# Turning the attention probabilities with VectorE and a trip through memory, in place of TensorE

## The chip, the core and the metric

The kernel runs on one core of a Trainium2 chip. The core has TensorE (PE, matmuls, with the loading of weights shown apart as PEld), VectorE (DVE), ScalarE (ACT), GpSimd (POOL) and SyncE (SP), which here only issues DMAs. Each engine works through its own list of instructions in the order in which they stand; semaphores hold an instruction until what it reads is there. The metric is the device time of one execution in microseconds. Comparisons are made between runs on one chip.

## The reference, cut to what matters

One encoder layer on 512 tokens of width 2048: a modulated RMS norm, one input projection, two token mixers side by side (attention with 16 heads of 64, and a gated linear attention), gates, an output projection, and a last RMS norm. The change touches the attention alone. For each head the reference forms logits, a softmax, and a product with the values:

```
s = jnp.einsum('bnqrhe,bnkrhe->bhrnqk', qb, kw).astype(jnp.float32) * (E ** -0.5)
...
m = jnp.max(s, axis=-1, keepdims=True)
p = jnp.exp(s - m)
den = jnp.sum(p, axis=-1, keepdims=True)
o = jnp.einsum('bhrnqk,bnkrhe->bhrnqe', (p / den).astype(v.dtype), vw)
```

The three dilated patterns are merged with weights from their denominators. The kernel does this with one dense 512 by 512 table per head: the bias table `g` holds, for each distance, the shared bias and the log of how many patterns reach it, so one softmax over all 512 keys gives the merged result.

## The kernel before, in words

All matrices are float32, kept as a high part and a low part (float32r), and each product is three matmuls (L169 to L171). The projection runs in units of 512 output columns. A unit reads eight weight groups of 512 KB (`raw`, four slots, L286); ACT makes the high part of each (L313), DVE the low part (L297), and PE runs 192 matmuls of 128x128 on 128x512 per unit, 24 per group.

Four units, `qk2`, `qk4`, `qk6` and `gk`, carry the attention beside their own matmuls: `unit` takes a list of side items with a place between 0 and 1, and emits each between the unit's matmuls when that share of them is out; items at 1 or more go to the next unit. So PE's list is written out by hand (PE is scheduled manually). The lists of DVE, ACT, POOL and SP are ordered by the framework's scheduler from the order of emission and its own view of when things are ready, side items first.

Each of these units does four heads, each head four tiles of 128 queries against 512 keys, so 16 tiles per unit and 64 in all. Names in the program carry head and tile: `p62` is head 6, tile 2; two tiles make a half, `pt50` and `o50` are head 5, half 0. A tile goes through these steps:

- score: two matmuls `s` on PE (L576, L577); DVE adds the bias row `g` and takes the row minimum (L580, CUSTOM_DVE_ANT in the profile, ISA in the program's list, with a second short row that reads the minimum out); ACT takes the exponential and its sum (L583); DVE the reciprocal (L584); POOL scales the row (L585).
- turn, two tiles later: four PE transposes into PSUM (`t`, L597); ACT makes the high part (L601) and DVE the low part (L602) of the turned tile in `pt`.
- values, per half: eight matmuls `o` on PE (L611); ACT copies one part out (L614); DVE adds the two into `cat` (L618).

At the end of such a unit `qk_evict` (L531) takes the new heads' queries and keys out of PSUM: eight ACT copies and eight DVE operations of 64x512 (L540, L550), and eight small DMAs. `g_load` fetches a head's bias table through SP (L564). `some_sums` puts conditioning sums of 128x1024 (L244, L680) and their loads beside the matmuls; 8 of the 48 lie in `qk6` and `gk`. Pools: `t2` has 16 tiles of 128x512 (queries, keys and score tiles), `b8` eight of 8 KB a row, `pa` three PSUM banks shared by `s`, `t` and `o`.

## Time and profile before

| | |
|---|---|
| median of 3 runs | 957.51 us (955.98 to 957.8) |
| profiled execution | 959.9 us, of which the span from first to last instruction is 957.9 us |
| granted clock | 0.997 |
| PE busy | 939.7 us, 98% of the span |
| DVE, ACT, POOL busy | 605.3, 431.5, 81.1 us |
| the units qk2, qk4, qk6, gk | 191.9 to 257.3, to 323.0, to 390.3, to 457.5 us |

In the profile's timeline a row gives start, duration, engine, line, operation, output and inputs, shape, and in brackets the idle time before it with what ended it. Groups of instructions give the count, the busy time in all, the mean in ns of one, and the idle time before them. The view by windows gives each engine's busy time in a stretch. Durations of operations that follow each other on one engine overlap a little, so the distance of two starts is what one costs its engine.

### The profile page before, as it was taken

To read this page: it belongs to the slowest core of one execution; us is meant where nothing else is said; L and a number is where in the kernel's file an instruction comes from. 1 tells how busy PE (TensorE), PEld (TensorE's weight loads), DVE (VectorE), ACT (ScalarE), POOL (GpSimd) and SP (SyncE) were. 2 spreads that over 40 slices of the span, in tenths; PEclk is the share of its full clock that TensorE was granted. 3 is DMA by queue.
4 is the path that set the end of the run, shared out by engine and by line. 5 is a ranking of instruction groups with operands and counts; after the bars stand their busy time and mean duration, and the time that the engine had idled before them with its cause. 6 is when DMAs were issued, how large, how long until landed. Compare 5 with 4: busy or idle time off the path is not lost.

```text
span 957.9 us, 11999 instructions
## 1 busy us (share of the span) xinstructions
PE 939.7 (98%) x4464; PEld 777.1 (81%) x4464; DVE 605.3 (63%) x900; ACT 431.5 (45%) x719; POOL 81.1 (8%) x100
## 2 busy tenths in 40 slices
PE   8999999999999999999999999999999999999996
PEld 5888788888888888888778888888887888888884
DVE  7988899675756676766435656675964352546421
ACT  5443533565655655655215544543834152233222
POOL 0000000012122022122000000000010000202120
PEclk9999999999999999999999999999999999999998
DMA  9999687443333463533454244354555464244013
GB/s 330 413 411 365 229 296 275 150 131 105 112 103 105 144 200 108 173 127 103 150 176 146 86 132 154 132 176 154 173 195 183 132 221 154 92 151 152 23 55 121
DMA packets 45180, 163.76 MB, mean 171 GB/s; under 512 B 5730, under 2 KB 6018, under 8 KB 40386
## 3 DMA queue, kind: packets, MB, share of 16 engines
q1 hardware_dynamic: 44946, 162.68, 49.9%
q8 instruction: 35, 0.57, 0.2%
q10 hardware_dynamic: 176, 0.33, 0.1%
q14 instruction: 23, 0.18, 0.1%
HBM read 154.51 MB, written 4.28 MB: 166 GB/s over the span
## 4 chain that ended last, share of the span: by engine, by line
PE 84%; DMA 6%; DVE 5%; issue 3%; ACT 1%; SPq 0%; POOL 0%; ACTq 0%; DVEq 0%; POOLq 0%
PE ps_o L170 6%; PE ps_o L169 6%; PE ps_o L171 6%; DMA rawg<-in_wg 6%; PE ps_qk L170 5%; PE ps_qk L169 5%; PE ps_qk L171 5%; PE o L611 3%; PE sta L169 3%; PE sta L170 3%; PE sta L171 3%; PE stb L171 3%; PE stb L169 3%; PE stb L170 3%; PE ps_gv L171 3%; PE ps_gv L170 3%
## 5 line engine op out<-in xcount | busy, mean ns | idle before, releaser
L585 POOL TENSOR_SCALAR p<-p,st 128x512 f32<-128x512 f32 x64 | 45.5, 711 | 406.6 <-DVE st L584 357.9
L244 DVE CUSTOM_DVE_ANT_0 cb<-cb,sb,c_bcond 128x2048 f32<-128x2048 f32 (+1 forms) x32 | 73.4, 2294 | 0.0
L583 ACT ACTIVATE p<-p,st 128x512 f32<-128x512 f32 x64 | 46.1, 721 | 56.8 <-DVE st L580 56.3
L602 DVE TENSOR_TENSOR pt<-t,pt 128x512 fp32r<-128x512 f32 x64 | 44.0, 689 | 16.2 <-ACT pt L601 15.8
L580 DVE CUSTOM_DVE_ANT_0 p<-s,g 128x512 f32<-128x512 f32 x64 | 43.6, 687 | 14.8 <-PE s L577 14.5
L601 ACT ACTIVATE pt<-t 128x512 fp32r<-128x512 f32 x64 | 37.8, 592 | 10.2 <-PE t L597 9.2
L244 DVE CUSTOM_DVE_ANT_0 rawg<-rawg,sb,gate 128x1024 f32<-128x1024 f32 x16 | 20.5, 1283 | 29.6 <-DMA rawg<-in_wg 29.6
L611 PEld LDWEIGHTS o<-pt,vv 128*128 128x128 f32 x256 | 34.7, 188 | 5.0 <-DVE pt L602 2.2
L597 PEld LDWEIGHTS t<-c_ident,p 128*128 128x128 f32 x256 | 31.8, 140 | 8.5
L597 PE MATMUL t<-c_ident,p 128*128 128x128 f32 x256 | 38.3, 272 | 0.0
L611 PE MATMUL o<-pt,vv 128*128 128x256 f32 x256 | 36.6, 283 | 0.9 <-DVE pt L602 0.8
L244 DVE CUSTOM_DVE_ANT_0 rawg<-rawg,sb,c_bcond 128x1024 f32<-128x1024 f32 x16 | 20.5, 1283 | 26.3 <-DMA rawg<-in_wg 26.3
L1014 POOL TENSOR_TENSOR x<-x,fgain 128x512 f32<-128x512 f32 x12 | 20.3, 1696 | 185.3 <-ACT ysq L1012 185.3
L1012 ACT ACTIVATE ysq<-x 128x512 f32<-128x512 f32 x16 | 10.1, 632 | 47.2 <-DVE x L1010 47.2
L767 POOL TENSOR_SCALAR dc<-st,sc 128x256 f32<-128x256 f32 x16 | 10.4, 652 | 245.5 <-DVE st L764 240.6
L1009 DVE TENSOR_TENSOR y<-ps_o,sb 128x512 f32<-128x512 f32 x16 | 10.9, 684 | 25.9 <-PE ps_o L171 25.9
L584 DVE RECIPROCAL st<-st 128x1 f32<-128x1 f32 x64 | 10.3, 162 | 24.9 <-ACT p L583 24.9
L576 PE MATMUL s<-ks,qs 128*128 128x512 f32 x64 | 25.1, 391 | 0.0
L577 PE MATMUL s<-kl,qs 128*128 128x512 f32 x64 | 25.0, 391 | 0.0
L774 ACT ACTIVATE sq<-st,sc 128x256 f32<-128x256 f32 x24 | 12.2, 509 | 26.8 <-DVE st L769 14.3
L1010 DVE TENSOR_TENSOR x<-y,x 128x512 f32<-128x512 f32 x16 | 18.0, 1125 | 0.3
L614 ACT ACTIVATE oh<-o 64x256 f32<-64x256 f32 x32 | 12.2, 382 | 13.0 <-PE o L611 12.2
(1275 smaller groups left out, 2916.7 us busy)
## 6 DMA issues: line engine op xcount, KB each, us to landing
cb<-in_wm SPq DMA_DIRECT2D x31, 1024.0 KB, 7.9
rawg<-in_wg SPq DMA_DIRECT2D x32, 512.0 KB, 3.4
raw_o<-in_w_o SPq DMA_DIRECT2D x32, 512.0 KB, 3.4
raw_qk<-in_w_qk SPq DMA_DIRECT2D x24, 512.0 KB, 3.4
rawb<-in_w_sb SPq DMA_DIRECT2D x16, 512.0 KB, 4.8
rawv<-in_wv SPq DMA_DIRECT2D x16, 512.0 KB, 3.8
raw_gv<-in_w_gv SPq DMA_DIRECT2D x16, 512.0 KB, 3.5
raw_ag<-in_w_ag SPq DMA_DIRECT2D x16, 512.0 KB, 3.3
```

The lines of the kernel that those rows point to most:

```text
L169: mm(ps, lh, rh, start=first, stop=False)
L170: mm(ps, ll, rh, start=False, stop=False)
L171: mm(ps, lh, rl, start=False, stop=last)
L244: nc.vector.tensor_tensor_reduce(out=w, in0=w, in1=with_, op0=ALU.mult, op1=ALU.add, scale=1.0, scalar=init, accum_out=dst)
L576: mm(ps, qs[:, q], ks, start=True, stop=False)
L580: nc.vector.tensor_tensor_reduce(out=t, in0=ps, in1=gt[h][:, P * i:P * i + 512], op0=ALU.add, op1=ALU.min, scale=1.0, scalar=3e38, accum_o ...
L583: act(t, t, AF.Exp, bias=st[:, 0:1], scale=-1.0, accum_out=st[:, 1:2])
L585: nc.gpsimd.tensor_scalar(t, t, st[:, 2:3], 1.0, op0=ALU.mult, op1=ALU.mult)
L597: nc.tensor.transpose(pk[:, kt * P:kt * P + P], t[:, kt * P:kt * P + P], ident)
L601: act(hi, src, AF.Copy)
L602: tt(lo, src, hi.bitcast(F32), op=ALU.subtract)
L611: mm(po[:, :256], vv[h // 4][:, kt, h % 4, :], t[:, w, kt, :], start=kt == 0 and w == 0, stop=kt == 3 and w == 1)
```

## The change

The turn on PE is taken out. `score` ends after the exponential; `scale` does the reciprocal and POOL's scaling. `turn` is now one VectorE transpose per tile (L602 of the changed kernel, STREAM_TRANSPOSE in the program's list), which turns each 32x32 block in its place and sorts the blocks by key range. `leave` writes the tile to a scratch buffer in memory (`away`, 256 KB); `back` reads a half back with four DMAs that put each block row on its partitions (`pf`, 512 KB, in a `raw` slot, in runs of 512 bytes). `parts` makes high and low parts of a whole half (128x1024) from `pf`, and `values` follows as before.

Each step has its own place: with x the number of the tile in the unit, score at x, scale x + 0.45, turn x + 0.9, leave x + 1.5, and for the half that ends with x, back x + 2.9, parts x + 4.6, values x + 7.0; one step of x is 0.0555 of a unit, from 0.13 on. So the last values of a unit fall into the next one. Beside it, the 8 sums leave `qk6` and `gk` (3 more in `gv0`, 3 in `gv1`, 1 in `ag0`, 1 in `gg1`), the weights are fetched one group less ahead in these four units, `cat` is allotted later, the row of shifts moves from 0.05 to 0.6 of `qk6`, and a small tensor `lrs` is split into two tiles of `t2`.

```diff
--- before.py
+++ after.py
@@ -70,12 +70,12 @@
 
 
 
-ATT_AT = (0.17, 0.8, 0.04, 0.05, 0.05)
+ATT_AT = (0.13, 0.0555)
 
 GLA_AT = (0.01, 0.02, 0.33, 0.46, 0.46, 0.56, 0.64, 0.76, 0.76, 0.88)
 GLA_FIRST = 0.2
 
-SUMS_IN = {"qk6": 4, "gk": 4, "gv0": 9, "gv1": 2, "ag0": 7, "ag1": 9, "gg0": 9}
+SUMS_IN = {"gv0": 12, "gv1": 5, "ag0": 8, "ag1": 9, "gg0": 9}
 
 
 def _plan(tasks, free, ready):
@@ -556,7 +556,7 @@
     def attention(pairs):
 
         tiles = [(2 * p + j, i) for p in pairs for j in range(2) for i in range(4)]
-        gt, pt, pr_ = {}, {}, {}
+        gt, pt, pr_, away, pf = {}, {}, {}, {}, {}
         heads = [2 * p + j for p in pairs for j in range(2)]
 
         def g_load(h):
@@ -566,8 +566,6 @@
 
         def score(h, i):
             def go():
-                if h % 8 == 0 and i == 0:
-                    cat[h // 8] = B8(f"cat{h // 8}", [4, 512])
                 if i == 1 and h != heads[-1]:
                     g_load(h + 1)
                 qs, ks, kl, _ = stacks[h]
@@ -581,29 +579,59 @@
                     out=t, in0=ps, in1=gt[h][:, P * i:P * i + 512], op0=ALU.add, op1=ALU.min,
                     scale=1.0, scalar=3e38, accum_out=st[:, 0:1])
                 act(t, t, AF.Exp, bias=st[:, 0:1], scale=-1.0, accum_out=st[:, 1:2])
+                pr_[h, i] = t, st
+            return go
+
+        def scale(h, i):
+
+            def go():
+                t, st = pr_.pop((h, i))
                 nc.vector.reciprocal(st[:, 2:3], st[:, 1:2])
                 nc.gpsimd.tensor_scalar(t, t, st[:, 2:3], 1.0, op0=ALU.mult, op1=ALU.mult)
+                half, ii = divmod(i, 2)
+                if ii == 0:
+                    away[h, half] = dp.tile([2, P, 512], F32, tag=f"away{h}{half}", name=f"away{h}{half}")
                 pr_[h, i] = t
             return go
 
         def turn(h, i):
+
+
             def go():
-                half, ii = divmod(i, 2)
-                if ii == 0:
-                    pt[h, half] = B8(f"pt{h}{half}", [2, 4, 256], F32R)
-                t = pr_.pop((h, i))
-                pk = PA(f"t{h}{i}")
-                for kt in range(4):
-                    nc.tensor.transpose(pk[:, kt * P:kt * P + P], t[:, kt * P:kt * P + P], ident)
-                hi = pt[h, half][:, 0, :, P * ii:P * ii + P]
-                lo = pt[h, half][:, 1, :, P * ii:P * ii + P]
-                src = pk.rearrange("p (k q) -> p k q", k=4)
+                t = T2(f"pt{h}{i}")
+                nc.vector.transpose(t.rearrange("p (b k r) -> p k b r", b=4, k=4), pr_.pop((h, i)))
+                pr_[h, i] = t
+            return go
+
+        def leave(h, i):
+            def go():
+                nc.sync.dma_start(away[h, i // 2][i % 2], pr_.pop((h, i)))
+            return go
+
+        def back(h, half):
+
+            def go():
+                t = away.pop((h, half))
+                f = RAW(f"pf{h}{half}", [8, 128])
+                for b in range(4):
+                    nc.sync.dma_start(f[32 * b:32 * b + 32], bass.AP(
+                        t.tensor, t.offset + P * b, [[512, 32], [32 * 512, 8], [1, P]]))
+                pf[h, half] = f
+            return go
+
+        def parts(h, half):
+            def go():
+                t = pt[h, half] = B8(f"pt{h}{half}", [2, 4, 256], F32R)
+                src = pf.pop((h, half)).rearrange("p b (k r) -> p k b r", k=4)
+                hi, lo = [t[:, e].rearrange("p k (b r) -> p k b r", b=8) for e in range(2)]
                 act(hi, src, AF.Copy)
                 tt(lo, src, hi.bitcast(F32), op=ALU.subtract)
             return go
 
         def values(h, half):
             def go():
+                if h % 8 == 0 and half == 0:
+                    cat[h // 8] = B8(f"cat{h // 8}", [4, 512])
                 t = pt.pop((h, half))
                 po = PA(f"o{h}{half}")
                 for kt in range(4):
@@ -620,20 +648,21 @@
 
         items = []
         n = len(tiles)
-        for x in range(n + 4):
-            if x < n:
-                items.append(score(*tiles[x]))
-            if 2 <= x <= n + 1:
-                items.append(turn(*tiles[x - 2]))
-            if 3 <= x <= n + 2 and tiles[x - 3][1] % 2 == 1:
-                items.append(values(tiles[x - 3][0], tiles[x - 3][1] // 2))
+        for x in range(n):
+            if True:
+                items.append((x, score(*tiles[x])))
+                items.append((x + 0.45, scale(*tiles[x])))
+                items.append((x + 0.9, turn(*tiles[x])))
+                items.append((x + 1.5, leave(*tiles[x])))
+                if tiles[x][1] % 2 == 1:
+                    h, half = tiles[x][0], tiles[x][1] // 2
+                    items.append((x + 2.9, back(h, half)))
+                    items.append((x + 4.6, parts(h, half)))
+                    items.append((x + 7.0, values(h, half)))
+        items.sort(key=lambda v: v[0])
         g_load(heads[0])
-        start, span, move0, move1, move_last = ATT_AT
-        at = [start + (q + 0.5) / len(items) * span for q in range(len(items))]
...
-        return list(zip(at, items))
+        start, step = ATT_AT
+        return [(start + step * x, go) for x, go in items]
 
     def gate_half(m, z):
 
@@ -854,7 +883,7 @@
                 todo = list(range(gi[name, gorder[0] if name == "o3" else 0], upto[name, g] + 1))
                 for i in todo:
                     split_hi(i)
-                for ahead in (1, 2):
+                for ahead in (1, 2)[:1 if name[:2] in ("qk", "gk") else 2]:
                     fetch(upto[name, g] + ahead)
             if i0 not in low:
                 split_lo(i0)
@@ -900,27 +929,29 @@
     for p in range(2):
         qk_evict(p, psb["b", 4 + 2 * p], psb["b", 5 + 2 * p])
     for n, p in (("qk2", 0), ("qk4", 2), ("qk6", 4)):
-        ps = unit(n, False, attention((p, p + 1)) + ([(0.05, shift_row)] + some_sums(n) if p == 4 else []))
+        ps = unit(n, False, attention((p, p + 1)) + ([(0.6, shift_row)] if p == 4 else []))
         for q in range(2):
             qk_evict(p + 2 + q, ps[2 * q], ps[2 * q + 1])
 
-    ps = unit("gk", False, attention((6, 7)) + some_sums("gk"))
+    ps = unit("gk", False, attention((6, 7)))
     gla["k"] = B8("gkt", [4, 512])
     for i in range(4):
         act(gla["k"][:, i, :], ps[i], AF.Copy)
 
 
-    lrb = B8("lrb", [KT, 32])
+    lrb = T2("lrb").rearrange("p (k c) -> p k c", k=KT)
     nc.sync.dma_start(lrb, a["w_lr"][0])
-    lrs = B8("lrs", [KT, 2, 32], F32R)
-    act(lrs[:, :, 0, :], lrb, AF.Copy)
-    tt(lrs[:, :, 1, :], lrb, lrs[:, :, 0, :].bitcast(F32), op=ALU.subtract)
+    lrs = [T2(f"lrs{e}", F32R).rearrange("p (k e c) -> p k e c", k=8, e=2) for e in range(2)]
+    for e in range(2):
+        src = lrb[:, 8 * e:8 * e + 8, :]
+        act(lrs[e][:, :, 0, :], src, AF.Copy)
+        tt(lrs[e][:, :, 1, :], src, lrs[e][:, :, 0, :].bitcast(F32), op=ALU.subtract)
     plr = PA("plr")
 
     def lr_tick(n):
         if n % 2 == 1:
             k = n // 2
-            w = lrs[:, k, :, :].rearrange("p a b -> p (a b)")
+            w = lrs[k // 8][:, k % 8, :, :].rearrange("p a b -> p (a b)")
             mm(plr[:64], w, h_hi[:, k, :], start=k == 0, stop=False)
             mm(plr[:64], w, h_lo[:, k, :], start=False, stop=k == KT - 1)
 
```

Three places of the lists show what moved. First DVE in the middle of `qk4`, around head 6 (the numbers behind the names only tell buffers apart). Before:

```order
L580 ISA p62_2502,st62_2503<-s62_2499,g6_2332 128x512
L580 ISA st62_2503 128x1
L297 TENSOR_TENSOR qk47l_2607<-raw_qk47_2437,qk47h_2606 128x1024
L584 RECIPROCAL st62_2503<-st62_2503 128x1
L602 TENSOR_TENSOR pt60_2511<-t60_2512,pt60_2511 128x4x128
L618 TENSOR_TENSOR cat0_1549<-o51_2527,oh51_2536 64x256
L580 ISA p63_2549,st63_2550<-s63_2546,g6_2332 128x512
L580 ISA st63_2550 128x1
L584 RECIPROCAL st63_2550<-st63_2550 128x1
L602 TENSOR_TENSOR pt60_2511<-t61_2558,pt60_2511 128x4x128
L580 ISA p70_2571,st70_2572<-s70_2568,g7_2472 128x512
```

and with the change:

```order
L628 TENSOR_TENSOR pt41_2410<-pf41_2356,pt41_2410 128x1024
L578 ISA p62_2512,st62_2513<-s62_2509,g6_2332 128x512
L578 ISA st62_2513 128x1
L646 TENSOR_TENSOR cat0_1774<-o41_2497,oh41_2506 64x256
L297 TENSOR_TENSOR qk46l_2458<-raw_qk46_2383,qk46h_2457 128x1024
L589 RECIPROCAL st62_2513<-st62_2513 128x1
L602 STREAM_TRANSPOSE pt62_2532<-p62_2512 128x4x4x32
```

which is followed at once by

```order
L578 ISA p63_2537,st63_2538<-s63_2534,g6_2332 128x512
L578 ISA st63_2538 128x1
L589 RECIPROCAL st63_2538<-st63_2538 128x1
L602 STREAM_TRANSPOSE pt63_2567<-p63_2537 128x4x4x32
L628 TENSOR_TENSOR pt50_2484<-pf50_2416,pt50_2484 128x1024
L646 TENSOR_TENSOR cat0_1774<-o50_2569,oh50_2578 64x256
L578 ISA p70_2584,st70_2585<-s70_2581,g7_2465 128x512
```

Before, between the minimum of a tile and the next tile's stands the reciprocal and the low part of a tile that is two tiles older. With the change the tile's own transpose stands there, which reads what POOL has scaled after this reciprocal; `pt41` and `pt50` (L628) are the low parts of whole halves, and `cat` of `o50` stands right behind `pt50`.

Second PE at the same place. Before:

```order
L170 MATMUL ps_qk4_3_2147<-h_hi_150,qk44l_2344 128x512
L171 MATMUL ps_qk4_3_2147<-h_lo_151,qk44h_2343 128x512
L597 MATMUL t60_2512<-c_ident_1459,p60_2428 128x128 x4
L169 MATMUL ps_qk4_0_2144<-h_hi_150,qk45h_2434 128x512
L170 MATMUL ps_qk4_0_2144<-h_hi_150,qk45l_2435 128x512
L171 MATMUL ps_qk4_0_2144<-h_lo_151,qk45h_2434 128x512
L611 MATMUL o51_2527<-pt51_2446,vv1_1064 128x256 x8
L169 MATMUL ps_qk4_0_2144<-h_hi_150,qk45h_2434 128x512
L170 MATMUL ps_qk4_0_2144<-h_hi_150,qk45l_2435 128x512
```

and with the change:

```order
L169 MATMUL ps_qk4_1_2088<-h_hi_150,qk45h_2380 128x512
L170 MATMUL ps_qk4_1_2088<-h_hi_150,qk45l_2381 128x512
L171 MATMUL ps_qk4_1_2088<-h_lo_151,qk45h_2380 128x512
L639 MATMUL o41_2497<-pt41_2410,vv1_1064 128x256 x8
L574 MATMUL s62_2509<-ks30_2073,qs30_2067 128x512
L575 MATMUL s62_2509<-kl30_2074,qs30_2067 128x512
L169 MATMUL ps_qk4_2_2089<-h_hi_150,qk45h_2380 128x512
L170 MATMUL ps_qk4_2_2089<-h_hi_150,qk45l_2381 128x512
```

The transposes are gone, and the score `s62` stands right behind the values `o41`, which read the parts `pt41` of the fence above.

Third SP at the border of `qk2` and `qk4`. Before (the bias table `g4` is far ahead of the moves of the keys):

```order
L564 DMA g4_2142<-grow_145 128x896
L286 DMA raw_qk44_2193<-in_w_qk4 128x1024
L564 DMA g5_2211<-grow_145 128x896
L286 DMA raw_qk45_2260<-in_w_qk4 128x1024
L549 DMA ks20_2112<-ks20_2112 64x512
L551 DMA kl20_2113<-kl20_2113 64x512
L549 DMA ks21_2118<-ks21_2118 64x512
L551 DMA kl21_2119<-kl21_2119 64x512
```

and with the change:

```order
L549 DMA ks30_2073<-ks30_2073 64x512
L608 DMA away31_2020<-pt33_2104 128x512
L551 DMA kl30_2074<-kl30_2074 64x512
L549 DMA ks31_2079<-ks31_2079 64x512
L551 DMA kl31_2080<-kl31_2080 64x512
L564 DMA g4_2085<-grow_145 128x896
L286 DMA raw_qk42_2094<-in_w_qk4 128x1024
L617 DMA pf30_2099<-away30_1948 32x8x128 x4
```

The write of tile `pt33` now stands ahead of the last moves of the keys (`kl30`, `ks31`, `kl31`), and these ahead of `g4`, which the first tile of `qk4` needs.

3 lines of the change are left out of this document (removed).

## The prediction

> **What bounds the kernel now.** I read the page's busy times first, then the view by windows of the four units that carry the attention.
>
> ```profile
> PE 939.7 (98%) x4464; PEld 777.1 (81%) x4464; DVE 605.3 (63%) x900; ACT 431.5 (45%) x719; POOL 81.1 (8%) x100
> ...
> core 0: us, PE busy (x) PEld busy (x) DVE busy (x) ACT busy (x) POOL busy (x), PEclk, DMA share, GB/s
> 191.90:257.30 65.40, 65.37 (x346) 54.89 (x345) 43.50 (x90) 38.81 (x75) 11.15 (x16) 1.00 0.37 113
> 257.30:323.00 65.70, 65.67 (x350) 55.34 (x349) 41.26 (x88) 36.80 (x71) 11.17 (x16) 1.00 0.36 107
> 323.00:390.30 67.30, 67.27 (x358) 56.45 (x357) 47.91 (x101) 38.23 (x75) 11.13 (x16) 1.00 0.52 162
> 390.30:457.50 67.20, 66.36 (x353) 55.91 (x352) 44.98 (x94) 36.50 (x70) 12.05 (x16) 1.00 0.42 132
> ```
>
> PE has no gap in these units; DVE works some 41 to 48 of 66 us. So PE sets their length, and what is taken off PE is won as long as no other list becomes longer. What the turn costs PE is read from starts, in the timeline of PE late in qk2:
>
> ```profile
> 249.40 0.39 PE L170 MATMUL ps_qk<-h_hi,qk27l 128*128 128x512 f32 x1
> 249.63 0.39 PE L171 MATMUL ps_qk<-h_lo,qk27h 128*128 128x512 f32 x1
> 249.86 0.60 PE L597 MATMUL t<-c_ident,p 128*128 128x128 f32 x4
> 250.22 0.48 PE L169 MATMUL ps_qk<-h_hi,qk27h 128*128 128x512 f32 x1
> 250.53 0.39 PE L170 MATMUL ps_qk<-h_hi,qk27l 128*128 128x512 f32 x1
> ```
>
> A matmul costs 0.23 us (249.40 to 249.63). The turn and the matmul behind it take 249.86 to 250.53, 0.67, so the turn costs 0.44, and 64 of them 28.2 us. That is all that the change can win. Per unit PE would fall from 66.4 (the mean of the four) to 59.4 us, 3.7 us for a tile.
>
> **The loop that the change closes on DVE.** DVE's list decides. With the change, each tile's transpose stands between its reciprocal and the next tile's minimum, so DVE runs minimum, wait for ACT, reciprocal, wait for POOL, transpose, and only then takes the next tile. Before, POOL's scaling lay outside DVE's list. The timeline of qk2 has every link:
>
> ```profile
> 206.78 0.69 DVE L602 TENSOR_TENSOR pt<-t,pt 128x512 fp32r<-128x512 f32 x1
> ...
> 207.39 0.68 DVE L580 CUSTOM_DVE_ANT_0 p<-s,g 128x512 f32<-128x512 f32 x1
> ...
> 208.11 0.72 ACT L583 ACTIVATE p<-p,st 128x512 f32<-128x512 f32 x1 [0.47 <-DVE st L580]
> ...
> 208.96 0.16 DVE L584 RECIPROCAL st<-st 128x1 f32<-128x1 f32 x1 [0.28 <-ACT p L583]
> 209.11 0.69 DVE L580 CUSTOM_DVE_ANT_0 p<-s,g 128x512 f32<-128x512 f32 x1
> 209.29 0.70 POOL L585 TENSOR_SCALAR p<-p,st 128x512 f32<-128x512 f32 x1 [1.75 <-DVE st L584]
> ...
> 209.84 0.72 ACT L583 ACTIVATE p<-p,st 128x512 f32<-128x512 f32 x1 [0.91 <-DVE st L580]
> ...
> 210.69 0.16 DVE L584 RECIPROCAL st<-st 128x1 f32<-128x1 f32 x1 [0.88 <-ACT p L583]
> ...
> 543.21 0.48 POOL L767 TENSOR_SCALAR dc<-st,sc 128x256 f32<-128x256 f32 x1 [3.19 <-DVE st L764]
> ...
> 543.73 0.48 DVE L769 SCALAR_TENSOR_TENSOR st<-kv,sc,dc 128x256 f32<-128x256 f32 x1 [0.71 <-POOL dc L767]
> ```
>
> Minimum to exponential 0.73 (209.11 to 209.84); exponential to reciprocal 0.85 (209.84 to 210.69); reciprocal to POOL 0.33 (208.96 to 209.29); POOL 0.70; POOL's end to DVE 0.04 (543.69 to 543.73). The transpose itself is in no row. From below it costs the DVE rows of the same 128x512 float32 tile, which stand 0.61 apart (206.78 to 207.39); from above the slowest row that this engine has for 512 columns:
>
> ```profile
> L717 DVE TENSOR_TENSOR_SCAN b<-rst,g 128x512 f32<-128x512 f32 x4 | 4.9, 1225 | 0.1
> ```
>
> That is 1.23 us, against the 0.69 at 206.78. I take 0.61 from start to start: a transpose has one input and no carried value, so the plain row is the nearer. The loop is then 0.73 + 0.85 + 0.33 + 0.70 + 0.04 + 0.61 = **3.26 us** a tile, with nothing else in it.
>
> The Trainium skill, VectorE: DVE Perf Modes, section The three transpose paths, gives 311 ns for a 128x128 bf16 turn of blocks on VectorE. Four such for our tile would be 1.24 us, an estimate by that page, near the scan's row; no run shown here has the instruction, and by that the sum would be the third rival's.
>
> **What else stands in the loop.** The low parts of weights, the low parts of halves and the additions into cat are in the same list, some in the waits, some not. Rows for them:
>
> ```profile
> 213.50 0.69 DVE L580 CUSTOM_DVE_ANT_0 p<-s,g 128x512 f32<-128x512 f32 x1 [1.01 <-PE s L577]
> ...
> 214.19 1.23 DVE L297 TENSOR_TENSOR qk25l<-raw_qk,qk25h 128x1024 fp32r<-128x1024 f32 x1
> ...
> 215.34 0.15 DVE L584 RECIPROCAL st<-st 128x1 f32<-128x1 f32 x1
> ...
> 451.91 1.29 DVE L602 TENSOR_TENSOR pt<-t,pt 128x512 fp32r<-128x512 f32 x2
> ...
> 452.65 1.10 PE L611 MATMUL o<-pt,vv 128*128 128x256 f32 x7 [0.84 <-DVE pt L602]
> 453.60 0.40 PE L169 MATMUL ps_gk<-h_hi,gk7h 128*128 128x512 f32 x1
> ...
> 454.27 0.42 DVE L618 TENSOR_TENSOR cat<-o,oh 64x256 f32<-64x256 f32 x1 [1.07 <-ACT oh L614]
> ```
>
> A 128x1024 difference costs 1.15 (214.19 to 215.34). Between minimum and reciprocal it makes that distance 0.61 + 1.15 = 1.76 instead of 1.58: 0.18; together with a cat (0.42 long, 0.36 from start to start) 0.54. Parts of a half are the same shape, as is the output of ACT's high part, which hides behind DVE's waits; they stand behind a transpose and cost 1.15 whole. Where their own cat follows at once, DVE also waits for the values: the first low part ends at 452.60, cat starts at 454.27, 1.67 later; with the 0.07 by which 1.22 outlasts 1.15 and cat's 0.36, 2.10 more. Where the next score stands behind those values on PE (s62 behind o41), the next minimum starts 0.05 + 0.95 + 0.23 + 0.39 + 0.04 = 1.66 after the low part: 1.73 more. PE has by then finished all before these values, since it needs 7.4 us for a pair that takes DVE some 10.
>
> At a border between units DVE has the last minimum, reciprocal and transpose, eight evictions, two parts, one weight, a cat and a cat behind its own parts.
>
> ```profile
> L540 DVE SCALAR_TENSOR_TENSOR qs<-ps_qk,qs 64x512 fp32r<-64x512 f32 x12 | 8.3, 689 | 0.4
> ...
> 196.89 0.69 DVE L540 SCALAR_TENSOR_TENSOR qs<-stb,qs 64x512 fp32r<-64x512 f32 x1 [0.66 <-ACT qs L539]
> ...
> 256.65 0.46 SPq L549 DMA_DIRECT2D ks<-ks  x1
> ...
> 215.45 0.33 SPq L286 DMA_DIRECT2D raw_qk<-in_w_qk  x1
> ...
> g<-grow SPq DMA_DIRECT2D x16, 448.0 KB, 4.4
> out<-x SPq DMA_DIRECT2D x16, 256.0 KB, 2.6
> ks<-ks SPq DMA_DIRECT2D x16, 128.0 KB, 2.2
> ```
>
> That is 0.61 + 0.16 + 0.61 + 8 x 0.62 + 2 x 1.15 + 1.15 + 0.36 + 2.10, and some 0.8 for waits on ACT's copies (an estimate from the 0.66 at 196.89): 13.1. On SP the write of the last tile waits for its transpose, 9.25 into this, and ahead of the next bias table stand that write (0.33) and three key moves (0.46 each): the table is issued at about 11.6 and lands 4.4 later, at 16.0, 2.9 after DVE is ready.
>
> **The sum.** Unit qk4, minimum of its first tile to that of the next unit's: 15 tiles at 3.26, 48.9; weights 4 x 0.18 + 2 x 0.54 + 1.15 = 2.95; six parts 6.9; three cats behind their own parts and one score behind values 3 x 2.10 + 1.73 = 8.0; border 13.1 + 2.9. **82.8 us**, where PE needs 59.4. Unit qk6 has the same pieces: 82.8. Unit qk2 has no parts in its first six tiles, and two of its four lie in waits: 48.9 + 0.9 + 0.2 + 2.3 + 5.3 + 16.0 = 73.6. Unit gk to its last minimum, without a border: 66.8. Together 306.0.
>
> ```profile
> L580 DVE CUSTOM_DVE_ANT_0 p<-s,g x64: 672/691/693, 200.6 to 448.9; 128x512 f32<-128x512 f32 x64
> ```
>
> Before, the first and the last minimum are 248.3 us apart: 57.7 lost. Behind them four values instead of two fall after the last score, less three turns (+0.6), and PE waits for lrs, which stands behind the last transpose (about 2): 2.5. So 60.2 on the profiled execution's 959.9 gives 1020.1; the median of the runs shown is 2.4 lower: **1018 us**.
>
> The rest I cost at nothing. Writes, 64 of 256 KB, and reads, 128 of 128 KB, add two times 16.8 MB over 306 us, 110 GB/s, to the 107 to 162 of the windows; a write takes 2.6 and a quarter read about 2.2 us (rows above), and between turn and parts lie over two tiles, 7 us and more. If they came late, each of the 32 halves would hold DVE: 32 us for each us; no gain is possible from it. One group less of weights ahead: a group is still asked for one group's use, 7.4 us, ahead, and the table of nearly that size lands in 4.4; if it came late, some 0.7 a unit. The moved sums, each a 128x1024 row like the 1.23 at 214.19, go into units behind the attention where PE's matmuls cover them; with that cover gone, 8 x 1.23 = 10.
>
> **Rivals.**
> 1. DVE's list keeps pace and PE stays the bound: 957.5 - 28.2 = 929. For it: DVE's busy time, 177.6 us over the four windows (the sum of their DVE columns), loses 64 low parts and 8 sums, gains 32 wider parts and 64 transposes, and comes to 52 of 59 us a unit. Against it: 3.26 of 3.7 us are taken by a loop that leaves 0.44 for the rest of a tile's work, which is over 1 us. Chance 0.08, with all that ends faster.
> 2. The loop holds, but the values and the table are never waited for: without 2.9 at three borders, without 14 x 1.74 behind cats and 6.3 behind scores, 979. For it: in the units before, DVE hardly waits for values. Against it: there the parts were made a tile ahead of the values, and now DVE's list puts cat right behind the parts. Chance 0.16, from 970 to 997.
> 3. The transpose costs the scan's 1.23: 0.54 more in some 60 tiles, 32 us: 1050. Chance 0.10.
> 4. PE slows when it has to wait. The trace has matmuls at its start that stand wider apart:
>
> ```profile
> 16.25 0.63 PE L169 MATMUL sta<-sa0h,h_hi 128*128 128x512 f32 x1
> 16.68 0.57 PE L170 MATMUL sta<-sa0h,h_lo 128*128 128x512 f32 x1
> 17.09 0.39 PE L171 MATMUL sta<-sa0l,h_hi 128*128 128x512 f32 x1
> ```
>
> They are 0.43 us apart (16.25 to 16.68), where later ones are 0.23. If the values and the score ran so at each of the 18 places where DVE waits for them, that is 0.95 + 0.23 at 1.87 times, 1 us more each: 1036. If all of a unit's 59.4 us did, it would be 111, PE would be the bound, and the time 957.5 + 4 x (111 - 66.4) = 1136. Against it: the values behind PE's 0.84 us of waiting at 452.65 run at the usual 0.95 (452.65 to 453.60); PE would now wait some 2.7 us a pair, for which there is no row. Chance 0.08. The Trainium skill, TensorE: Matmul & The Clock Gate, Part 1, has PE fall to half its clock after an idle window of about 3.4 us; by that rule most of these waits are just too short and the time stays near the forecast; the trace's first matmuls agree with the half.
>
> Forecast: 0.56, own range 998 to 1040. No change: 0.02, where gain and waits cancel. So faster by over 0.2% (about what this kernel's timing can tell) 0.08, within 0.02, slower 0.90. The range 975 to 1055 takes in the forecast, most of rival 2, and most of 3 and 4.
>
> **What would show it.** DVE's longest wait in these units becomes the transpose's on POOL, near 0.9 us each; minima some 4 to 5 us apart; PE busy about 59 of 74 to 83 us per unit, idle ahead of o; transposes at 0.69. Wrong if these units are shorter than before, if PE's idle ends on DMA, or if the loss lies in a later stage.

## The result

| | median, us | lowest to highest | ratio to before | 95% interval |
|---|---|---|---|---|
| before | 957.65 | 955.98 to 958.27 | 1 | |
| changed | 1031.37 | 1028.66 to 1036.6 | 1.0779 | 1.0735 to 1.0824 |

The change makes the kernel 74 us slower. It lies inside the predicted range, on the side that was forecast, 13 us above the predicted 1018. The profiled execution of the changed kernel took 1028.66 us, its span is 1026.8.

The page's first rows, and the view of the groups by line, of the changed kernel:

```profile
PE 943.3 (92%) x4208; PEld 768.8 (75%) x4208; DVE 640.4 (62%) x933; ACT 426.0 (41%) x688; POOL 79.9 (8%) x100
...
L602 DVE STREAM_TRANSPOSE pt<-p 128x512 f32<-128x512 f32 x64 | 45.5, 711 | 47.6 <-POOL p L590 47.5
L628 DVE TENSOR_TENSOR pt<-pf,pt 128x1024 fp32r<-128x1024 f32 x32 | 38.2, 1195 | 3.6 <-ACT pt L627 3.6
```

PE was busy 98% and is now busy 92%. The busy sum did not even fall, although 256 transposes left PE: matmuls that ran at a lower clock stand longer in it. The transposes' row has 47.5 us of DVE waiting for POOL ahead of them.

The view by windows, cut at the first minimum of each unit (the last window ends at the last minimum; columns as before):

```profile
200.60:278.00 77.40, 65.19 (x281) 52.10 (x280) 45.02 (x91) 31.58 (x58) 11.09 (x16) 0.93 0.61 169
278.00:363.60 85.60, 67.53 (x292) 53.78 (x291) 50.25 (x97) 36.21 (x64) 11.09 (x16) 0.92 0.69 183
363.60:451.20 87.60, 69.41 (x287) 54.89 (x286) 50.44 (x96) 36.63 (x65) 11.09 (x16) 0.88 0.70 188
451.20:518.30 67.10, 52.59 (x232) 41.75 (x231) 39.02 (x80) 26.84 (x49) 10.39 (x15) 0.95 0.72 196
```

From first to last minimum it is 317.6 us where it was 248.3; behind the last minimum it is 508.5 (1026.8 - 518.3) where it was 509.0. So the whole loss lies in the four units. No engine is full in them: DVE is busy 50 of 86 us, PE 68, and the granted clock is 0.88 to 0.95 where it was 1.00.

DVE's timeline in qk2, one turn of the loop with nothing else in it, and the view of DVE's waits from 200 to 520 us (what waited, for what: sum, times, longest):

```profile
210.99 0.65 DVE L578 CUSTOM_DVE_ANT_0 p<-s,g 128x512 f32<-128x512 f32 x1
211.57 0.08 DVE L578 DVE_READ_ACCUMULATOR2_ANT st<- 128x1 f32 x1
212.59 0.16 DVE L589 RECIPROCAL st<-st 128x1 f32<-128x1 f32 x1 [0.93 <-ACT p L581]
213.57 0.71 DVE L602 STREAM_TRANSPOSE pt<-p 128x512 f32<-128x512 f32 x1 [0.82 <-POOL p L590]
214.21 0.65 DVE L578 CUSTOM_DVE_ANT_0 p<-s,g 128x512 f32<-128x512 f32 x1
```

```profile
DVE pt L602 <- POOL p L590: 47.5, 59, 0.9
DVE st L589 <- ACT p L581: 34.9, 41, 0.9
DVE cat L646 <- ACT oh L642: 28.7, 14, 2.7
DVE p L578 <- DMA g<-grow: 9.4, 3, 3.6
DVE p L578 <- PE s L575: 8.1, 7, 1.8
```

Minimum to minimum is 3.22 (210.99 to 214.21): 1.60 to the reciprocal, 0.98 to the transpose, 0.64 to the next minimum. The waits of the loop, 47.5 and 34.9, are the two largest; those for values, table and score (28.7, 9.4, 8.1) are the next. PE's waits in the same stretch:

```profile
PE o L639 <- ACT pt L627: 27.7, 17, 4.6
PE o L639 <- DVE pt L628: 25.8, 20, 1.7
PE ps_qk L170 <- DVE qk25l L297: 2.0, 1, 2.0
```

PE waited 53.5 us ahead of the values and, over all such rows, 9.4 for parts of weights. Before, it waited 0.8 and 0 for them in this stretch.

### The profile page after: what moved, and what is told of

Same layout as the page of the kernel before. It is cut to its first block, busy times and chain, and to the rows that moved or that the text cites. A ratio compares the mean times of both kernels' runs of the same rounds, so it can differ in the third digit from the quotient of the medians.

```text
span 1026.8 us, 11784 instructions
## 1 busy us (share of the span) xinstructions
PE 943.3 (92%) x4208; PEld 768.8 (75%) x4208; DVE 640.4 (62%) x933; ACT 426.0 (41%) x688; POOL 79.9 (8%) x100
## 4 chain that ended last, share of the span: by engine, by line
PE 41%; issue 7%; DMA 6%; DVE 6%; POOL 1%; ACT 1%; SPq 0%; ACTq 0%; DVEq 0%; POOLq 0%
PE ps_o L171 6%; PE ps_o L170 6%; PE ps_o L169 6%; PE ps_gg L169 3%; PE ps_gg L171 3%; PE ps_gg L170 3%; DMA rawg<-in_wg 3%; PE ps_gv L169 2%; DMA rawv<-in_wv 2%; PE ps_gv L170 2%; PE ps_gv L171 2%; PE go L834 1%; PE ps_ag L169 1%; PE ps_ag L170 1%; PE ps_ag L171 1%
## 5 line engine op out<-in xcount | busy, mean ns | idle before, releaser
L639 PE MATMUL o<-pt,vv 128*128 128x256 f32 x256 | 50.0, 331 | 55.6 <-ACT pt L627 29.0
L639 PEld LDWEIGHTS o<-pt,vv 128*128 128x128 f32 x256 | 40.0, 218 | 69.7 <-ACT pt L627 36.9
L602 DVE STREAM_TRANSPOSE pt<-p 128x512 f32<-128x512 f32 x64 | 45.5, 711 | 47.6 <-POOL p L590 47.5
L628 DVE TENSOR_TENSOR pt<-pf,pt 128x1024 fp32r<-128x1024 f32 x32 | 38.2, 1195 | 3.6 <-ACT pt L627 3.6
L646 DVE TENSOR_TENSOR cat<-o,oh 64x256 f32<-64x256 f32 x32 | 13.2, 412 | 35.2 <-ACT oh L642 35.1
L627 ACT ACTIVATE pt<-pf 128x1024 fp32r<-128x1024 f32 x32 | 33.4, 1045 | 0.1
L589 DVE RECIPROCAL st<-st 128x1 f32<-128x1 f32 x64 | 10.3, 160 | 34.9 <-ACT p L581 34.9
L1043 ACT ACTIVATE ysq<-x 128x512 f32<-128x512 f32 x16 | 10.1, 631 | 47.3 <-DVE x L1041 47.3
L796 POOL TENSOR_SCALAR dc<-st,sc 128x256 f32<-128x256 f32 x16 | 10.4, 649 | 248.3 <-DVE st L793 243.4
L1040 DVE TENSOR_TENSOR y<-ps_o,sb 128x512 f32<-128x512 f32 x16 | 10.9, 684 | 25.9 <-PE ps_o L171 25.9
```

Of the source, the lines that this page charges most:

```text
L602: nc.vector.transpose(t.rearrange("p (b k r) -> p k b r", b=4, k=4), pr_.pop((h, i)))
L627: act(hi, src, AF.Copy)
L628: tt(lo, src, hi.bitcast(F32), op=ALU.subtract)
L639: mm(po[:, :256], vv[h // 4][:, kt, h % 4, :], t[:, w, kt, :], start=kt == 0 and w == 0, stop=kt == 3 and w == 1)
```

## The experiments

All of these kernels compute the whole result. The number behind x is the place in the order in tiles: a turn at x + 1.2 is emitted behind the score of tile x + 1. "Units" is first to last minimum, and "PE busy" how long PE was busy in that stretch; the last two columns are PE's waits between 200 and 520 us, ahead of values and for parts of weights, each the sum of the rows of that view. The kernel before was measured beside each of them, so differences between two runs are taken by their ratios ("by the ratios").

| kernel | median | ratio to before, interval | units | PE busy | values | weights |
|---|---|---|---|---|---|---|
| before | 957.65 | 1 | 248.3 | 248.2 | 0.8 | 0 |
| changed | 1031.4 | 1.0779 (1.0735 to 1.0824) | 317.6 | 254.6 | 53.5 | 9.4 |
| e1 turn later | 1005.6 | 1.0484 (1.0437 to 1.0530) | 291.2 | 247.3 | 43.2 | 2.0 |
| e3 scale on VectorE | 1019.4 | 1.0648 (1.0622 to 1.0674) | 308.8 | 253.9 | 47.3 | 9.2 |
| e5 table ahead | 1026.1 | 1.0710 (1.0692 to 1.0727) | 314.8 | 256.1 | 49.8 | 10.5 |
| e4 values later | 1027.8 | 1.0744 (1.0714 to 1.0773) | 317.3 | 258.1 | 1.2 | 54.6 |
| e6 turn and values later | 1019.3 | 1.0660 (1.0640 to 1.0680) | 301.9 | 248.0 | 0 | 56.2 |
| e7 both, table ahead | 1017.7 | 1.0638 (1.0622 to 1.0654) | 302.0 | 250.0 | 2.6 | 51.5 |
| e8 weights earlier too | 979.5 | 1.0224 (1.0208 to 1.0240) | 263.4 | 239.4 | 23.8 | 2.1 |
| e11 loop put back | 1015.1 | 1.0580 (1.0557 to 1.0603) | 297.2 | 249.7 | 41.2 | 0.6 |
| e2 the moves alone | 959.0 | 1.0011 (0.9997 to 1.0025) | 248.2 | 248.1 | 1.1 | 0 |
| e9 four of eight by VectorE | 951.6 | 0.9931 (0.9919 to 0.9944) | 243.8 | 236.5 | 0 | 0 |
| e10 three of eight | 946.4 | 0.9879 (0.9866 to 0.9893) | 238.3 | 237.7 | 0.6 | 0 |
| e12 four of eight, opened | 942.8 | 0.9836 (0.9822 to 0.9849) | 236.0 | 234.4 | 0.3 | 0 |

The turn was priced at 28.2 us of PE, so the work left to PE in this stretch should take 248.2 - 28.2 = 220.0 us. Where a part of the turns stays on PE and PE hardly waits, the price holds: 237.6 follows for e10 (five of eight on PE) and 234.1 for e12 (four), 237.7 and 234.4 were measured. In every kernel that makes PE wait, PE is busy for longer than its work explains, 254.6 instead of 220.0 in the changed one: matmuls behind waits ran at a lower granted clock.

### e1: the turn behind the next minimum

```diff
-                items.append((x + 0.9, turn(*tiles[x])))
+                items.append((x + 1.2, turn(*tiles[x])))
```

> One number is changed: the turn of a tile stands behind the next tile's minimum in VectorE's list (x + 1.2 instead of x + 0.9). Work, transfers and matmuls are the same. Theory of the loop: the waits on ACT and POOL no longer stand between two minima; a tile then takes VectorE the 0.73 + 0.85 from minimum to reciprocal and 0.16 for it, with the turn (0.64) inside that wait, 1.74 plus parts, weights and cat, some 3.2 in the mean, less than the 3.7 that TensorE needs. Units of 60 to 66 us, 930 to 965 us in all, some 945. Rival, the work: VectorE has too much to do with turns and parts, in whatever order: 1015 or more. Rival, the trip over memory: 1020 or more, and ACT's high part waits for its transfer.

Measured 1005.6, some 28 us less by the ratios, where 86 less was expected. The loop did open, as DVE's waits from 200 to 510 us show:

```profile
DVE p L578 <- PE s L575: 33.7, 30, 1.9
DVE cat L646 <- ACT oh L642: 24.7, 16, 2.8
DVE pt L628 <- ACT pt L627: 13.2, 16, 2.2
...
DVE st L589 <- ACT p L581: 8.7, 31, 0.3
DVE pt L602 <- POOL p L590: 3.8, 6, 0.8
```

DVE's waits for POOL fell from 47.5 to 3.8 and those for the exponential from 34.9 to 8.7: 70 us. But its waits for scores rose from 8.1 to 33.7, and it now waits 13.2 for high parts. PE still waited 43.2 ahead of values. So the loop was a cause, and not the only one: a second hold-up lay right behind it. The trip over memory is one of its links: on the page of e1 the chain of work that ended last runs through the reads `pf` for 5% of the span, some 50 us, and ACT waited 5.1 us for them, where it waited 1.0 in the changed kernel.

### e2: the moves without the turn

The kernel before, with the change's SUMS_IN, its one group of look-ahead, its place of shift_row and its two lrs tiles. The turn stays on PE.

> The kernel before with only the moves around the turn: the eight sums out of qk6 and gk, the shift at 0.6, one group less of weights ahead, lrs in two tiles; the turn stays on TensorE. Theory of the loop, where these are covered: 957.5, within 4 of it. Rival, that the moved sums or the later weights carry a part of the loss of 74: 967 to 980.

1.0011, at most 1.0025: 2.4 us. PE waits 1.1 us in the units. The moves around the turn carry at most 2.4 of the 74. The later place of `cat` is not in this run.

### e3: the scaling on VectorE

```diff
-                nc.gpsimd.tensor_scalar(t, t, st[:, 2:3], 1.0, op0=ALU.mult, op1=ALU.mult)
+                nc.vector.tensor_scalar(t, t, st[:, 2:3], 1.0, op0=ALU.mult, op1=ALU.mult)
```

> The changed kernel with the scaling of the weights on VectorE instead of POOL, 64 instructions of some 0.65 us more in VectorE's list. Theory of the loop: from reciprocal to transpose 0.98 becomes 0.10 + 0.65, 0.23 less for a tile, less what used to fill the waits: 1018 to 1025. Rival, the work on VectorE sets the time: 64 x 0.65 more, 1073. Rival, the trip over memory sets it: no change, 1031.

1019.4, as the loop has it. DVE has 64 instructions more, and the kernel is 12 us faster: the free tiles of qk2 stand 2.90 to 2.97 apart instead of 3.16 to 3.23. A scaling takes DVE 0.49 us (31.1 for the 64), less than the 0.65 expected. This excludes that DVE's work as such sets the time; what counts is what its list stands still for. Nor does the trip over memory set it alone: that is unchanged, and the time fell.

### e5: the table ahead

The list of tables becomes one for all units, and the second tile of a unit's last head asks for the next unit's first table:

```diff
-                if i == 1 and h != heads[-1]:
+                if i == 1 and h != 15:
...
-        g_load(heads[0])
+        if heads[0] == 0:
+            g_load(0)
```

> The changed kernel with the first bias table of a unit asked for in the unit before, when the last head's table is in use, instead of behind the border's key moves. Theory of the border as predicted: the three waits for the table (9.4 us in the trace) go, since the scores they stand before are done 3.1 to 3.5 us earlier: 1022. Rival, that a wait for the next pair's values or transfers takes its place: 1028 to 1031.

1026.1, between the two: some 6.6 us by the ratios. From last to first minimum over a border took 15.4 or 15.5 instead of 18.0 to 18.9, 9 us in the three. Most of it came back, and the units together are only 2.8 us shorter: the second distance of the next unit grew from 7.4 to 9.9, 8.4 and 8.6. There ACT now waits for the reads of a pair (2.2, 0.9 and 0.9 us), and DVE behind ACT. The wait moved by one tile, from the table to the trip over memory.

### e4 and e6: the values two tiles later

e4 is the changed kernel with this line, e6 has e1's line too:

```diff
-                    items.append((x + 7.0, values(h, half)))
+                    items.append((x + 9.0, values(h, half)))
```

> The changed kernel with the values of a pair two tiles later in TensorE's list (x + 9 instead of x + 7) and nothing else; the turn stays ahead of the next minimum. Theory of two couplings: the loop on VectorE (3.2 a tile) is one, and the values that TensorE takes up right behind their own low part, with a cat or a score queued behind them, are the other. This takes the second alone: VectorE's waits on cat (28.7) and on scores (8.1) go, TensorE's waits ahead of the values (53 in the trace) shrink with them, and the loop stays: 995 to 1005. Rival, the loop alone bounds the units and those waits only move: 1020 or more. Rival, VectorE and TensorE are both freed: below 975.

> Both edits, the turn behind the next minimum (x + 1.2) and the values two tiles later (x + 9). Theory of two couplings: with both gone TensorE's 59 to 62 a unit is the bound, apart from the borders: 940 to 965, minima 3 to 4 apart. Rival, VectorE's work (some 50 busy of a unit) with what is left of waits, 70 a unit: 975 to 985. Rival, the trip over memory, now with less time to hide in: 985 or more, with ACT's high parts waiting on transfers.

Both expectations fell. e4 took 1027.8, inside the noise of the changed kernel (its interval, 1.0714 to 1.0773, touches the other's), and e6 is 17 us slower than e1. PE's waits, first of e4:

```profile
PE ps_qk L169 <- ACT qk43h L313: 4.0, 1, 4.0
PE ps_qk L169 <- ACT qk63h L313: 4.0, 1, 4.0
PE ps_gk L169 <- ACT gk3h L313: 4.0, 1, 4.0
```

and of e6, in its timeline of PE between 316 and 328 us:

```profile
317.18 0.50 PE L170 MATMUL ps_qk<-h_hi,qk46l 128*128 128x512 f32 x1 [1.70 <-DVE qk46l L297]
...
326.59 0.50 PE L169 MATMUL ps_qk<-h_hi,qk47h 128*128 128x512 f32 x1 [2.02 <-ACT qk47h L313]
328.31 0.50 PE L170 MATMUL ps_qk<-h_hi,qk47l 128*128 128x512 f32 x1 [1.22 <-DVE qk47l L297]
```

PE no longer waits for values (1.2 and 0), it waits for parts of weights (54.6 and 56.2), where the changed kernel had 53.5 and 9.4. Only the operand has changed. Some half of these waits are for high parts, which ACT makes (25.2 and 27.0), the rest for low parts from DVE. DVE's list in e6 shows how the latter come about. It makes qk46l behind a minimum that waits for a score:

```profile
315.28 0.69 DVE L578 CUSTOM_DVE_ANT_0 p<-s,g 128x512 f32<-128x512 f32 x1 [1.20 <-PE s L575]
315.90 1.22 DVE L297 TENSOR_TENSOR qk46l<-raw_qk,qk46h 128x1024 fp32r<-128x1024 f32 x1
```

PE needs qk46l from 315.5 (317.18 less its wait of 1.70), and the low part is begun at 315.90, because the minimum ahead of it waited for PE. ACT's high parts come late in the same way: qk43h, for which PE waited 4.0, is begun at 289.27, behind an exponential that had waited 1.90 for DVE's minimum. So I read the two lists as running in step: each feeds the other with less distance than the other's longest hold-up, and passes its own hold-up on.

### e7: both edits and the table ahead

e6 with e5's edit.

> Both edits of the run before and the first bias table of each unit asked for in the unit before. Theory: at the borders VectorE is then held by its own evictions alone; 6 to 10 less than with both edits: 932 to 957. Rival, that the border is paid by TensorE's order (weights of the next unit before its first score), not by the table: within 2 of the run with both edits.

1017.7, within 2 of e6, as the rival has it. The borders did become 1.4 to 1.7 us shorter; in qk4 the five distances behind the border then grew from 22.9 to 24.1 together. With these two edits in place the table is worth next to nothing.

### e8: the parts of weights two groups ahead

```diff
-        upto[ug] = max([gi[x] for x in uses[:i + 2]])
+        upto[ug] = max([gi[x] for x in uses[:i + (3 if ug[0][:2] in ("qk", "gk") else 2)]])
```

> The run with both edits and the table ahead, and the parts of a group of weights begun two groups ahead of their matmuls instead of one, in the four units. In that run TensorE waited 51.5 us for parts of weights in these units and 2.6 for values, where the changed kernel had 9.4 and 53.5: the wait had only changed its operand. Theory of distances: each operand that VectorE makes must lie further ahead of its matmul than VectorE's longest hold-up; with the weights moved too, TensorE's waits there fall below 30 and the time to 985 to 995. Rival, VectorE's list is too slow a supplier in any order: the waits move on to the next operand, their sum stays at 50 or more, and the time at 1010 to 1020.

979.5, below what the theory of distances expected, 40 us less by the ratios than e7. PE's waits for weights are 2.1, those for values 23.8, and the sum has fallen from 54.1 to 25.9. The edit moves both parts of the weights ahead, and with them their transfer; but in e7 neither ACT nor DVE waited for a transfer of these weights, so it is the parts that count. DVE is busy 182 us in the stretch, as in e7 (183), so most of PE's waits in e7 were not for want of DVE's time; the operands had been made too late for their use.

### e11: the loop put back

e8 with the turn at x + 0.9 again, the reverse of e1's line.

> The run with the weights' parts earlier, with one number put back: the turn stands again ahead of the next minimum (x + 0.9). Everything else (values two tiles later, table ahead, weights' parts two groups ahead) stays mended. Theory that the closed loop is the dear part as soon as the other distances are long enough: a tile takes 3.2 and more again, 1005 to 1015, some 30 above that run. Rival, the loop costs only what it cost alone in the first comparison, where opening it gave 26 with the other distances short, or less: 980 to 1000. Rival, it costs nothing once operands lie far ahead: 979.

1015.1, 34 us above e8 by the ratios. DVE waits for POOL as it did in the changed kernel (here from 200 to 500 us):

```profile
DVE pt L604 <- POOL p L592: 47.2, 58, 0.9
DVE st L591 <- ACT p L583: 31.1, 38, 0.9
DVE cat L648 <- ACT oh L644: 21.8, 14, 2.9
```

With e1 that makes a square. Opening the loop is worth 28 with the other distances short, 34 with them long. Mending the other distances (values, table, weights) is worth 19 with the loop closed (1.0779 to 1.0580), 25 with it open (1.0484 to 1.0224). Both together are worth 53 of the 74.

### e9, e10 and e12: a part of the turns back on TensorE

Of the eight half heads of a unit, some are turned by TensorE with the code of the kernel before, under the name pturn, the rest by VectorE. The table is asked for ahead, and the parts of weights are made two groups ahead. e10 has, by half head:

```diff
+                if x // 2 in (0, 2, 4, 6, 7):
+                    items.append((x + 2.0, pturn(*tiles[x])))
+                    if tiles[x][1] % 2 == 1:
+                        items.append((x + 3.5, values(tiles[x][0], tiles[x][1] // 2)))
+                    continue
...
-                    items.append((x + 7.0, values(h, half)))
+                    items.append((x + 9, values(h, half)))
```

e9 has (0, 2, 4, 6) there, e12 (0, 2, 5, 7), VectorE's turn at x + 1.2 and four sums in gk.

> In each unit four of the eight half heads (every other one) are turned by TensorE as before the change, four by VectorE and over memory as in it; with the table ahead, the parts of weights two groups ahead, and the offsets set for this (turn 0.9, write 1.2, reads 2.5, parts 4.6, values 8; TensorE's turn 2.0, its values 3.5; first score at 0.08, step 0.052). Theory of distances: VectorE's own turns and its wider parts fall by half, TensorE gives back 14 us of the 28, and the two lists meet at 62 to 66 a unit: 945 to 960. Rival, any turn by VectorE holds up its list and TensorE behind it: half of the 74, 985 to 1000.

> As the run before with five of the eight half heads of a unit turned by TensorE and three by VectorE (parts 5.6, values 9, first score at 0.16, step 0.05). Theory of distances: TensorE's share is 17.6 us of turns, units of 62 to 65: 945 to 960, within 5 of the run with four. Rival, any turn by VectorE holds up its list: about 28 above before, 985.

> Half heads 0, 2, 5 and 7 of a unit turned by TensorE, the other four by VectorE, with VectorE's turn behind the next minimum (x + 1.2), parts at 6.1, values at 8.5 and 4 (TensorE's), first score at 0.16, step 0.05, and four of the moved sums back in gk. Theory: TensorE turns 14 instead of 17.6 us and stays the bound, units of 61 to 63: 940 to 946, at or a little below the run with three of eight. Rival, VectorE becomes the bound at four of eight whatever the order: 950 or more, as in the run with four.

951.6, 946.4 and 942.8: all three are faster than the kernel before, e12 by 1.6%, 15.5 us. The windows of e12, cut every 63 us:

```profile
200.00:263.00 63.00, 62.83 (x318) 52.68 (x317) 45.11 (x94) 35.65 (x66) 11.17 (x16) 1.00 0.57 157
263.00:326.00 63.00, 62.83 (x322) 52.81 (x321) 45.09 (x94) 36.84 (x69) 11.99 (x16) 1.00 0.64 188
326.00:389.00 63.00, 61.83 (x317) 51.67 (x316) 44.41 (x90) 36.65 (x69) 11.99 (x16) 1.00 0.63 181
389.00:436.00 47.00, 46.98 (x237) 39.30 (x236) 36.39 (x80) 25.83 (x49) 12.44 (x14) 1.00 0.68 221
```

PE is full again, at clock 1.00, in units of 61.3 to 64.4 us instead of 65.6 to 66.6. Half of the 28.2 us that the turn costs PE is 14.1; 12.3 of it shows in the units (248.3 - 236.0). With the same share of turns on VectorE, e9 and e12 differ by 9: e9 has the turn at x + 0.9, with 23.0 us of DVE's waits for POOL. It also differs in other offsets, so that not all of the 9 is the loop's.

## Why the prediction was right, step by step

**The bound.** That DVE's list would stand still, that PE would idle ahead of values, and that the transpose's wait for POOL would be DVE's largest, at 0.9 us each, is what the profile shows. One sign came out otherwise: PE was to be busy about 59 us of a unit, and was 65 to 69, at a granted clock of 0.88 to 0.93.

**The loop.** Predicted 3.26 a tile, measured 3.16 to 3.23 where nothing else stands in it. The links were off by little and in part against each other: 1.58 predicted from minimum to reciprocal and 1.60 measured, 1.07 and 0.98 from there to the transpose. The transpose costs 0.64 from start to start, where I took 0.61, and 0.71 in its own row, against the scan's 1.23. Rival 3 falls with that. The Trainium skill's 311 ns, VectorE: DVE Perf Modes, section The three transpose paths, gave 1.24 as an estimate for this tile; 0.71 was measured, and the measurement decides.

**What else stands in the loop.** Behind its own parts a cat waited 1.66 or 1.67 us at full clock (245.99, 255.88, 330.96), the predicted 1.67. A minimum behind values waited 1.66 at 321.20, the distance predicted from low part to score. The mechanism of these terms was right. Their number was right for cat (14 waits) and not for scores, 7 instead of 4.

**The sum.** By units, predicted and measured:

| | qk2 | qk4 | qk6 | gk | together |
|---|---|---|---|---|---|
| tiles, predicted | 57.6 | 66.8 | 66.8 | 66.8 | 258.0 |
| tiles, measured | 59.1 | 66.7 | 69.6 | 67.1 | 262.5 |
| border, predicted | 16.0 | 16.0 | 16.0 | | 48.0 |
| border, measured | 18.3 | 18.9 | 18.0 | | 55.2 |

The step that was mis-sized is the border, "13.1 + 2.9": 7.2 us in the three. The table still ended it, with waits of 3.2, 3.6 and 2.6 in place of the 2.9; but the table came later, and DVE too was ready later, after 15.1 to 15.4. The timelines of DVE and, below them, of SP at the first border, whose last minimum starts at 259.76:

```profile
261.93 0.69 DVE L540 SCALAR_TENSOR_TENSOR qs<-ps_qk,qs 64x512 fp32r<-64x512 f32 x1 [0.45 <-ACT qs L539]
262.65 0.68 DVE L550 TENSOR_TENSOR kl<-ps_qk,ks 64x512 fp32r<-64x512 f32 x1
...
270.23 0.71 DVE L602 STREAM_TRANSPOSE pt<-p 128x512 f32<-128x512 f32 x1
...
274.41 0.42 DVE L646 TENSOR_TENSOR cat<-o,oh 64x256 f32<-64x256 f32 x1 [2.36 <-ACT oh L642]
278.01 0.69 DVE L578 CUSTOM_DVE_ANT_0 p<-s,g 128x512 f32<-128x512 f32 x1 [3.18 <-DMA g<-grow]
```

```profile
270.98 0.34 SPq L608 DMA_DIRECT2D away<-pt  x1
271.41 0.46 SPq L551 DMA_DIRECT2D kl<-kl  x1
271.96 0.55 SPq L549 DMA_DIRECT2D ks<-ks  x1
272.61 0.55 SPq L551 DMA_DIRECT2D kl<-kl  x1
273.20 0.58 SPq L564 DMA_DIRECT2D g<-grow  x1
```

On the table's path, the last transpose starts 10.5 into the border, not 9.25; the table is issued 3.0 behind that, not some 2.4, since the write and the moves of keys stand 0.43 to 0.65 apart on SP, where the sum had 0.33 and 0.46; and it lands 4.8 later, not 4.4. In all three borders these three links came 3.7, 1.9 and 1.6 us later than forecast, which is the 7.2. The first of them is in good part the evictions: one takes 0.72 from start to start, not the 0.62 of the sum, 0.8 for eight. DVE's own path ends with a cat behind its own parts, which waited 2.36 instead of 1.67, since its values were slow; as the table came later still, that cost nothing here. PE's timeline, a little earlier at the same border:

```profile
260.68 0.39 PE L171 MATMUL ps_qk<-h_lo,qk40h 128*128 128x512 f32 x1
263.51 0.58 PE L639 MATMUL o<-pt,vv 128*128 128x256 f32 x1 [2.44 <-ACT pt L627]
264.77 1.86 PE L639 MATMUL o<-pt,vv 128*128 128x256 f32 x7 [0.68 <-DVE pt L628]
266.43 0.63 PE L169 MATMUL ps_qk<-h_hi,qk40h 128*128 128x512 f32 x1
266.86 0.63 PE L170 MATMUL ps_qk<-h_hi,qk40l 128*128 128x512 f32 x1
```

Behind 2.44 us of waiting the matmuls stand 0.43 apart, and seven matmuls of values take 1.86 instead of 1.10. This is rival 4 in part: it holds at 7 of the 32 values, most of them at or just behind a border, and there cat waited 2.2 to 2.7. Three of the seven stand at borders, where the table was later still; the other four, at some 0.8 us each, are some 3 of the 11.6 us by which the stretch is above the prediction, an estimate from those rows. Nearly all other values ran at 1.10. Two places with nearly the same waits fell apart: behind 1.08 and 1.50, at 327.46, the values took 1.10, behind 1.01 and 1.43, at 414.59, they took 1.66, so the wait alone does not decide. The Trainium skill, TensorE: Matmul & The Clock Gate, Part 1, has the clock fall after an idle window of some 3.4 us, and the windows run freely of the kernel. Free windows would let nearly equal waits end differently, as they did; that 2.44 us of waiting is enough is less than the page gives. The forecast's "just too short" held at most values and not at the borders.

The tail was to lose 2.5 and gained 0.5. So the span came out 68.9 above the old one, where 60.2 was predicted: 11.6 more in the units, 3.0 less behind them, two errors that lie against each other.

**What was costed at nothing.** The moved sums and the look-ahead cost 2.4 us at most (e2). The trip over memory stayed nearly covered in the changed kernel, though a read took 4.7 us where I took 2.2 from the key moves:

```profile
away<-pt SPq DMA_DIRECT2D x64, 256.0 KB, 2.3
pf<-away SPq DMA_DIRECT2D x128, 128.0 KB, 4.7
```

In all the units ACT waited 1.0 us for such a read. In e1, with the loop open, it was 5.1, and in e5 4.0. No run shortens the trip, so what a shorter one would gain, with the loop open above all, is not shown.

**What the sum did not say.** It is a sum along one list, and it says how long this order takes, not what each term would give if it were removed. My first expectations took it so, and fell: 86 for the loop was 28, 30 for the values nothing. Behind each hold-up stood another of nearly its size, since PE's list and DVE's feed each other. It took four edits together (turn, values, table, weights) to bring 53 of the 74 back. What holds e8 at 22 above before can be given as a balance of PE's time, from first to last minimum, before and in e8:

```profile
200.63:448.89 248.26, 248.17 (x1322) 208.97 (x1321) 164.55 (x351) 139.55 (x272) 43.92 (x63) 1.00 0.41 127
201.16:464.60 263.44, 239.43 (x1078) 195.75 (x1076) 181.65 (x358) 128.49 (x234) 45.26 (x62) 0.95 0.77 217
```

Of e8's 263.4 us, 220.0 are the work left to PE, 24.0 are idle, 21.8 of them ahead of values, and 19.4 are matmuls that ran slower, at a granted clock of 0.95. So PE's waits are paid twice, as idle time and in slower matmuls behind them, and the two together outweigh the 28.2 that the turn gave back. Why PE still waits there, with DVE waiting 34.8 ahead of cat, stays open. With half of the turns, in e12, PE waits 0.3 ahead of values and DVE 10.9 ahead of cat.

## What to carry to other kernels

Moving work off the bounding engine pays only if the engine that takes it can take it without standing still: look at what will stand ahead of and behind the new instruction in its list, and whose answer it waits for, before adding up busy times. When two in-order engines feed each other, give each operand more distance than the longest hold-up of its maker, all operands at once; mending one moves the wait to the next. And the share can be chosen: half of the turns moved gave 1.6% where all of them cost 7.8%, and still 2.2% in the best order tried. A wait of TensorE can also cost more than its length, since matmuls behind it ran slower here.

## What the runs showed of the hardware

- VectorE's transpose of a 128x512 float32 tile in blocks of 32 takes 0.71 us, 0.64 from start to start, close to this engine's other rows of that size (0.69 and 0.61 in the kernel before).
- TensorE's matmuls of 512 columns stood 0.43 us apart behind 2.44 us of waiting, for some 6.4 us. They slowed at each of the six places where a wait of 2.44 us or more stood ahead of values of the changed kernel. Behind waits of up to 1.56 they mostly stayed 0.23 apart; the one plain exception, at 414.59, had 1.01 and 1.43.
- In the kernels in which TensorE waited for over 20 us, its work between first and last minimum took 19 (e8) to 38 us (e4) longer than at full clock, an estimate from busy times and the turn's 28.2.
- A read of 128 KB from memory in runs of 512 bytes took 4.7 us to land, four issued together, and 3.0 in e10, where there were 48 in place of 128; a move of the same size between tiles of the core, in runs of 2 KB, took 2.2.
